# The rows of all engines ordered by the framework's other model, in a two-block transformer kernel

## The chip, the cores and the metric

The kernel runs on one core of a Trainium2 chip. The metric is device microseconds (us) of one execution. Times before: 2521.05, 2525.29 and 2524.74 us, median 2524.74.

## The reference

One sequence of 512 tokens with 1024 features goes through two blocks in float32:

```
first_block:  h = rms_norm(x); q, k, v, bg, cg, xc = split(h @ w_in)
              y_attn = chunked attention with relative bias and QK-norm (16 heads of 64)
              y_conv = bg * conv3(cg * xc)
              x += (sig(gates) * y_attn @ w_attn_proj + sig(gates) * y_conv @ w_conv_proj) @ w_out
              x += square(relu(rms_norm(x) @ w_up)) @ w_down
second_block: shift, scale, gate = split(silu(c) @ w_ada)
              stick-breaking attention (8 heads) and mLSTM (4 heads) side by side, then w_out_2
              PEER: top 16 of 128 x 128 experts for 8 heads; y = sum gate * gelu(h . u_e) * v_e
```

## The kernel before, in words

Activations lie feature-major: 8 tiles of 128 features by 512 tokens. Every float32 operand of a product is split into a rounded high part and a low part, and each product is three matmuls (`mm3`, lines 152 to 156: high-high, high-low, low-high) with 512 columns, 24 per output tile of 128 features (`linear`, line 158). Weights come in blocks of 1 MB: `weights` (line 136) loads a block into `wraw` on the SP queue (line 140), ACT casts it to `whi` (line 143) and DVE, or GpSimd for some blocks, subtracts to `wlo` (lines 145, 149). There are two buffers of each, and in the experts three of `whi` and `wlo` and two of `wraw`.

The stages, in the order of the code: `block1` (line 264) with the convolution branch, `attention` (line 556), the merge with the gates, and the MLP (`w_up`, `w_down`); `mix` (line 665) with `stick_breaking` (line 821) and `mlstm` (lines 921, 955); `peer` (line 1040) with the choice of experts (`select`, line 1238), the spreading of their gates over a table of all 16384 experts for the first 384 tokens (`spread`, line 1302), and `experts` (line 1363), which for these tokens runs through all experts in 128 chunks of 128. The last 128 tokens take another way: `row_experts` (line 1155) gathers the rows of each chosen expert by indirect DMA (line 1152, six buffers) and multiplies them on DVE (lines 1173, 1181) beside the chunks. The activations of the first 48 chunks are computed earlier (`ahead`, line 1111), between the steps of `select` and `spread`.

In the attention each head has four blocks of queries: PE makes scores into PSUM (line 596), DVE adds the bias and takes the maximum (line 598), ACT takes the exponential (line 110, called from `attention`), DVE scales (line 606), PE transposes (line 616), ACT and DVE split (lines 620, 621) and PE multiplies with the values (lines 550, 551). In stick-breaking, PE makes scores (lines 837, 839), ACT takes the absolute value, exponential and logarithm (lines 844, 110), DVE adds and splits (lines 847, 850, 851), PE adds the cumulative sums (lines 864 to 866), ACT takes the exponential (line 110), DVE splits the weights (lines 871, 872) and PE takes the values (lines 550, 551).

What sets the order: the code is traced from top to bottom without an order of its own for the engines. When the `with tile.TileContext(nc)` block (line 1554) closes, the framework makes the rows: it runs the traced program on a model of the chip, and each time an engine is free in that model it gives it, of the instructions that are possible then, the one that was traced first. Buffers are given out in the same run. The outcome is one fixed row per engine and DMA queue, which the chip then executes. So an instruction can be put ahead of many that were traced before it, if the model holds those back. The kernel limits this in places with edges that order two instructions without a wait: `behind` (line 115) adds one. The sums for `w_ada` (line 483) and the products of gathered rows (`later`, line 1160) are kept behind `self.pace`, an instruction of the main work that was traced shortly before them; the transposes that start `spread` are kept behind the last matmul of `ahead` (line 1321), and three early weight loads behind the load of an activation (line 142).

```
mm(out, wh, xh, start=start, stop=False)
mm(out, wh, xl, start=False, stop=False)
return mm(out, wl, xh, start=False, stop=stop)
...
kind = mybir.DependencyClass.Sync if sync else mybir.DependencyClass.NoSync
self.tc.add_manual_dep(i.ins, name, mybir.DependencyInfo(kind, mybir.DependencyReason.DATA), reason="keeps pace")
```

## Time and profile before

| what | value |
|---|---|
| median of 3 runs | 2524.74 us |
| the profiled execution's own time | 2522.37 us |
| its span, first to last instruction | 2520.6 us |
| TensorE (PE) matmuls busy | 2467.9 us, 98% |
| TensorE weight loads (PEld) busy | 2114.4 us, 84% |
| VectorE (DVE) busy | 1872.7 us, 74% |
| ScalarE (ACT) busy | 1056.6 us, 42% |
| GpSimd (POOL) busy | 624.1 us, 25% |
| DMA | 515 MB, mean 204 GB/s |

Busy time is the time in which an engine had at least one instruction in work; matmuls overlap, so the mean length of one is longer than its share of the busy time. The span is what the profile covers, and the execution's own time is 1.8 us longer. SP is the engine that issues most transfers; a wait of "SPq" is one of its queue.

### The profile page before, as it was taken

How to read it: one execution, taken by the hardware profiler on the slowest of the kernel's cores; microseconds unless marked ns; L12 is line 12 of the kernel's file. 1: busy time of each engine (PE TensorE's matmuls, PEld its weight loads, DVE VectorE, ACT ScalarE, POOL GpSimd, SP SyncE). 2: the span in 40 equal slices, each digit the busy share in tenths (PEclk: the TensorE clock that was granted, in tenths of full speed). 3: DMA queues.
4: the chain of work that ended last, by engine and by line, in shares of the span. 5: the costliest groups of instructions: out<-in, count | busy, mean ns of one | idle time of the engine just before them, and what ended most of it. 6: DMA issues, size and time to landing. Idle time of an engine off the chain costs nothing.

```text
span 2520.6 us, 33112 instructions
## 1 busy us (share of the span) xinstructions
PE 2467.9 (98%) x12655; PEld 2114.4 (84%) x12655; DVE 1872.7 (74%) x3094; ACT 1056.6 (42%) x1480; POOL 624.1 (25%) x506
## 2 busy tenths in 40 slices
PE   9999999999999999999999989999999999999999
PEld 7887887877888887777789988978889999999998
DVE  5558777855555557897779999857668787888887
ACT  5226555643222236766653345543333333333332
POOL 0001100111011001001035630011135555555552
PEclk9999999999999999999999999999999999999999
DMA  5352323443444332114343357799879999999995
GB/s 202 127 199 99 104 93 101 139 170 135 174 150 148 138 137 85 38 67 138 120 162 120 124 184 276 311 319 341 300 267 333 327 339 333 328 336 335 336 340 195
DMA packets 172312, 515.03 MB, mean 204 GB/s; under 512 B 13396, under 2 KB 78308, under 8 KB 146296
## 3 DMA queue, kind: packets, MB, share of 16 engines
q1 hardware_dynamic: 133960, 376.52, 42.6%
q0 software_dynamic: 37040, 135.35, 14.9%
q8 instruction: 99, 1.62, 0.2%
q10 hardware_dynamic: 1152, 1.05, 0.1%
q14 instruction: 61, 0.50, 0.1%
HBM read 461.47 MB, written 51.38 MB: 203 GB/s over the span
## 4 chain that ended last, share of the span: by engine, by line
PE 76%; DVE 15%; ACT 4%; DMA 2%; issue 2%; SPq 0%; POOL 0%; ACTq 0%; DVEq 0%; POOLq 0%
PE pa L154 12%; PE pa L156 12%; PE pa L155 12%; PE pp L1443 7%; PE pp L1442 7%; PE pp L1446 7%; PE pu L154 4%; PE pu L156 4%; PE pu L155 4%; DVE wlo L145 1%; ACT whi L143 1%; DVE tk_rest L1194 1%; PE pb L596 1%; DVE tk_e L1230 1%; DMA mg_a<-g_dram 1%
## 5 line engine op out<-in xcount | busy, mean ns | idle before, releaser
L143 ACT CAST whi<-wraw 128x2048 fp32r<-128x2048 f32 x229 | 437.6, 1911 | 540.6 <-PE pa L155 296.5
L145 DVE TENSOR_TENSOR wlo<-wraw,whi 128x2048 fp32r<-128x2048 f32 x210 | 489.0, 2329 | 125.7 <-ACT whi L143 119.3
L154 PE MATMUL pa<-hh,whi 128*128 128x512 f32 (+1 forms) x1360 | 523.0, 385 | 7.1 <-ACT whi L296 3.4
L156 PE MATMUL pa<-hh,wlo 128*128 128x512 f32 (+1 forms) x1360 | 516.4, 381 | 2.3 <-DVE wlo L145 2.2
L155 PE MATMUL pa<-lh,whi 128*128 128x512 f32 (+1 forms) x1360 | 518.4, 381 | 0.0
L1443 PE MATMUL pp<-wlo,hew 128*128 128x512 f32 x768 | 299.0, 390 | 1.5 <-DVE wlo L145 1.5
L1442 PE MATMUL pp<-whi,hew 128*128 128x512 f32 x768 | 298.7, 390 | 1.7 <-ACT hew L1409 1.1
L1152 POOL DMA_INDIRECT r_row<-in_u_rows,r_at x128 | 184.4, 1440 | 461.7 <-DVE r_w L1173 419.6
L154 PEld LDWEIGHTS pa<-hh,whi 128*128 128x128 f32 x1360 | 257.6, 190 | 47.0 <-ACT whi L296 3.6
L156 PEld LDWEIGHTS pa<-hh,wlo 128*128 128x128 f32 x1360 | 257.2, 189 | 44.6 <-issue 3.6
L155 PEld LDWEIGHTS pa<-lh,whi 128*128 128x128 f32 x1360 | 257.5, 189 | 40.9 <-issue 5.3
L1446 PE MATMUL pp<-whi,lew 128*128 128x512 f32 x768 | 237.1, 389 | 0.0
L1152 POOL DMA_INDIRECT r_row<-in_expert_v,r_at x128 | 194.0, 1516 | 173.2 <-DVE r_big L1181 135.7
L156 PE MATMUL pu<-hh,wlo 128*128 128x384 f32 x640 | 215.0, 336 | 0.0
L154 PE MATMUL pu<-hh,whi 128*128 128x384 f32 x640 | 215.0, 336 | 0.0
L155 PE MATMUL pu<-lh,whi 128*128 128x384 f32 x640 | 214.9, 336 | 0.0
L1446 PEld LDWEIGHTS pp<-whi,lew 128*128 128x128 f32 x768 | 144.1, 188 | 30.3
L1443 PEld LDWEIGHTS pp<-wlo,hew 128*128 128x128 f32 x768 | 144.1, 188 | 29.6 <-DVE wlo L145 2.3
L1442 PEld LDWEIGHTS pp<-whi,hew 128*128 128x128 f32 x768 | 144.1, 188 | 29.2 <-ACT hew L1409 1.3
L1181 DVE SCALAR_TENSOR_TENSOR r_big<-r_row,r_w,r_big 128x1024 f32<-128x1024 f32 x127 | 162.9, 1283 | 3.0
L1409 ACT CAST hew<-ex_w 128x384 fp32r<-128x384 f32 x128 | 65.5, 513 | 226.3 <-DVE ex_w L1405 149.1
L1173 DVE CUSTOM_DVE_ANT_0 r_row<-r_row,r_big 128x1024 f32<-128x1024 f32 x128 | 151.3, 1220 | 0.0
(440 smaller groups left out, 4480.1 us busy)
## 6 DMA issues: line engine op xcount, KB each, us to landing
wraw<-in_expert_u SPq DMA_DIRECT2D x64, 1024.0 KB, 7.4
wraw<-in_expert_v SPq DMA_DIRECT2D x64, 1024.0 KB, 7.6
wraw<-in_w_in SPq DMA_DIRECT2D x37, 1024.0 KB, 4.9
ada_w<-in_w_ada SPq DMA_DIRECT2D x24, 1024.0 KB, 4.8
gate_dram<-oh_s SPq DMA_DIRECT2D x12, 2048.0 KB, 7.0
ex_g<-gate_dram SPq DMA_DIRECT2D x31, 768.0 KB, 10.9
wraw<-in_w_up SPq DMA_DIRECT2D x16, 1024.0 KB, 5.3
wraw<-in_w_down SPq DMA_DIRECT2D x16, 1024.0 KB, 4.8
```

Source lines behind the costliest of these rows:

```text
L143: nc.scalar.copy(hi, raw)
L145: nc.vector.tensor_sub(lo, raw, hi.bitcast(F32))
L154: mm(out, wh, xh, start=start, stop=False)
L155: mm(out, wh, xl, start=False, stop=False)
L156: return mm(out, wl, xh, start=False, stop=stop)
L1152: self.nc.gpsimd.indirect_dma_start(t, None, src, at)
L1173: later(nc.vector.tensor_tensor_reduce(row, row, h, 1.0, 0.0, op0=ALU.mult, op1=ALU.add, accum_out=w[:, k:k + 1]))
L1181: later(nc.vector.scalar_tensor_tensor(acc, row, w[:, k:k + 1], acc, op0=ALU.mult, op1=ALU.add))
L1409: nc.scalar.copy(hi, w)
L1442: mm(sums[b][half], hi, v[0][:, c, hc], start=n == 0, stop=False)
L1443: mm(sums[b][half], hi, v[1][:, c, hc], start=False, stop=False)
L1446: mm(sums[b][half], lo, v[0][:, c, hc], start=False, stop=n == P - 1)
```

## The change

It gives the context that makes the rows one more argument, by which the program is run on the framework's timeline model instead of its default one. Kernel code, instructions, operands, buffers' numbers and edges stay. What can differ is the sequence in each engine's row and in each DMA queue, and the buffer that a tile gets.

```diff
--- before.py
+++ after.py
@@ -1551,7 +1551,7 @@
     I = {n: nc.dram_tensor("in_" + n, a.shape, mybir.dt.from_np(a.dtype), kind="ExternalInput").ap()
          for n, a in A.items()}
     y = nc.dram_tensor("out_y", (T // P, P, D), F32, kind="ExternalOutput").ap()
-    with tile.TileContext(nc) as tc:
+    with tile.TileContext(nc, schedule_with_timeline_sim=True) as tc:
         build(tc, I, y)
     r = run_bass_kernel_spmd(nc, [{"in_" + n: a for n, a in A.items()}], core_ids=[0])
     return np.ascontiguousarray(r.results[0]["out_y"].reshape(1, T, D))
```

## Rows read from the trace of the kernel before

**Rows 1.** The page's head, busy time, and the granted clock in 40 slices.

```profile
span 2520.6 us, 33112 instructions
...
PE 2467.9 (98%) x12655; PEld 2114.4 (84%) x12655; DVE 1872.7 (74%) x3094; ACT 1056.6 (42%) x1480; POOL 624.1 (25%) x506
...
PEclk9999999999999999999999999999999999999999
```

**Rows 2.** Busy time by stage: stretch, its length, busy us (instructions) of each engine.

```profile
core 0: us, PE busy (x) PEld busy (x) DVE busy (x) ACT busy (x) POOL busy (x), PEclk, DMA share, GB/s
0.00:190.00 190.00, 185.58 (x808) 152.93 (x809) 109.67 (x132) 62.59 (x66) 13.73 (x22) 0.99 0.49 177
190.00:500.00 310.00, 304.48 (x1610) 247.88 (x1610) 242.12 (x530) 177.97 (x349) 33.62 (x62) 1.00 0.30 103
500.00:600.00 100.00, 95.24 (x402) 75.59 (x400) 51.43 (x57) 43.21 (x52) 11.19 (x8) 0.98 0.50 180
600.00:940.00 340.00, 340.00 (x1493) 279.96 (x1492) 186.21 (x208) 87.85 (x79) 40.17 (x32) 1.00 0.40 144
940.00:1275.00 335.00, 316.62 (x1611) 254.98 (x1611) 267.73 (x416) 219.82 (x381) 28.79 (x36) 0.99 0.28 96
1275.00:1485.00 210.00, 206.17 (x1121) 188.63 (x1119) 190.71 (x869) 80.34 (x95) 118.18 (x90) 1.00 0.39 131
1485.00:1655.00 170.00, 162.08 (x1391) 149.20 (x1392) 143.46 (x128) 87.09 (x147) 9.07 (x6) 0.96 0.73 279
1655.00:2521.00 866.00, 857.78 (x4228) 765.20 (x4227) 681.36 (x757) 297.70 (x314) 369.31 (x250) 1.00 0.90 318
```

**Rows 3.** What TensorE waits for: total us, times, longest.

```profile
PE pb L1319 <- DVE pk_i L1236: 6.8, 1, 6.8
PE pd L550 <- DVE sb_wh L871: 5.7, 2, 3.4
PE pb L596 <- DVE at_st L598: 3.5, 4, 0.9
```

**Rows 4.** Busy time and granted clock of two stretches of 20 us.

```profile
1020.00:1040.00 20.00, 19.05 (x122) 16.64 (x120) 19.38 (x37) 15.31 (x28) 0.00 (x0) 1.00 0.16 54
1040.00:1060.00 20.00, 17.09 (x86) 13.64 (x86) 14.09 (x23) 11.68 (x21) 0.00 (x0) 0.91 0.08 22
```

**Rows 5.** Groups of instructions in the attention, 190 to 500 us: the softmax.

```profile
L110 ACT ACTIVATE at_e<-at_e,at_st 128x128 f32<-128x128 f32 (+1 forms) x64 | 35.9, 563 | 17.6 <-DVE at_st L600 17.5
...
L598 DVE CUSTOM_DVE_ANT_0 at_e<-pb,bias 128x128 f32<-128x128 f32 (+1 forms) x64 | 29.3, 481 | 0.9 <-PE pb L596 0.7
...
L606 DVE TENSOR_SCALAR at_e<-at_e,at_r 128x128 f32<-128x128 f32 (+1 forms) x64 | 21.1, 386 | 0.1
```

**Rows 6.** Groups of instructions in the mixer, 940 to 1275 us: stick-breaking.

```profile
L110 ACT ACTIVATE sb_l<-sb_l 128x512 f32<-128x512 f32 (+1 forms) x48 | 27.3, 592 | 0.6
...
L847 DVE SCALAR_TENSOR_TENSOR sb_l<-pb,sb_l 128x512 f32<-128x512 f32 (+1 forms) x24 | 15.1, 638 | 2.4 <-ACT sb_l L110 2.2
...
L844 ACT ACTIVATE sb_l<-pb 128x512 f32<-128x512 f32 (+1 forms) x24 | 13.2, 557 | 6.0 <-DVE sb_o L851 5.2 <-PE pb L839 0.8
L110 ACT ACTIVATE sb_w<-pb 128x512 f32<-128x512 f32 (+1 forms) x24 | 13.1, 554 | 1.6 <-DVE sb_wl L872 1.6
...
L871 DVE CAST sb_wh<-sb_w 128x512 fp32r<-128x512 f32 (+1 forms) x24 | 9.1, 394 | 0.0
```

**Rows 7.** Groups of instructions in the experts, 1660 to 2500 us.

```profile
L145 DVE TENSOR_TENSOR wlo<-wraw,whi 128x2048 fp32r<-128x2048 f32 x103 | 235.9, 2290 | 75.5 <-ACT whi L143 74.5
...
L143 ACT CAST whi<-wraw 128x2048 fp32r<-128x2048 f32 x103 | 197.0, 1913 | 190.3 <-PE pp L1446 86.2 <-PE pu L155 80.4 <-DMA wraw<-in_expert_v 21.8
...
L1181 DVE SCALAR_TENSOR_TENSOR r_big<-r_row,r_w,r_big 128x1024 f32<-128x1024 f32 x127 | 162.9, 1283 | 3.0
```

**Rows 8.** The page's DMA issues: size and us from issue to landing.

```profile
wraw<-in_expert_v SPq DMA_DIRECT2D x64, 1024.0 KB, 7.6
```

**Rows 9.** What DVE waits for in the experts, 1660 to 2500 us.

```profile
DVE wlo L145 <- ACT whi L143: 74.5, 60, 5.0
```

## The prediction

> **What bounds the kernel now.** I read the page's head first, then busy time by stage, then what TensorE waits for, and last the groups of the stages that wait. In the head [rows 1] the reader is to see one number: PE is busy for 2467.9 of 2520.6 us. TensorE is the bound, and 2520.6 - 2467.9 = 52.7 us is all that stands between the span and a TensorE that never rests. The change removes no instruction, so these 52.7 us are the only time that an order can give back, and it has no such limit in the other direction.
>
> The table by stage [rows 2] shows where the 52.7 us lie. From 600 to 940 us, the first block's MLP, PE is busy for 340.00 of 340. From 1655 us to the end, the experts, 857.8 of 866, and part of the missing 8.2 is the end itself. These two stages are 1206 us in which the order has next to nothing to give. Idle time sits in the others: 4.4 us at the start, 5.5 in the attention (190 to 500), 4.8 in the merge (500 to 600), 18.4 in the mixer (940 to 1275), 3.8 in the expert selection, 7.9 in the spreading of its gates (1485 to 1655). The waits [rows 3] name the longest of them: 6.8 us in one piece for the last index of the selection, a chain that no order shortens; 5.7 us in two pieces for the weights of stick-breaking; 3.5 us in four pieces for the running maximum of the attention. So the time sits in hand-offs: PE makes scores, ACT and DVE work on them, PE takes them up again, and other matmuls have to stand in the row meanwhile.
>
> **What the change does.** It adds and removes no instruction, no wait of the algorithm, no transfer. It changes the rows, that is, the sequence in which every engine and every DMA queue gets its instructions. Program order is the priority in both cases, and the NoSync edges (`behind`) hold in both; between instructions that are both possible, the model's clock decides which comes first. An engine takes its row strictly in sequence, so an instruction whose operand is late holds up all behind it. I cost it stage by stage.
>
> MLP and start: nothing. The work that covers any shift is there: DVE is busy for 186 of 340 us and ACT for 88 [rows 2], so both have slack of over 45% and weights are split long before PE wants them. If that cover went, one late split would cost at most one cast and one subtraction, 1.91 + 2.29 us by their groups in the experts [rows 7].
>
> Attention: one softmax block costs 0.481 us on DVE (score plus bias, with maximum), 0.563 us on ACT (exponential) and 0.386 us on DVE (scaling) [rows 5]: 1.43 us from PE to PE, 64 times. Fully hidden it costs nothing; fully exposed, 64 x 1.43 = 91.5 us. Now 5.5 us of it are exposed, 6%.
>
> Mixer: one stick-breaking block costs 0.557 + 2 x 0.592 us on ACT, 0.638 us on DVE (the cast after it is left out as partly parallel), then 0.554 on ACT and 0.394 on DVE before its values are taken [rows 6]: 3.33 us, 24 times, 79.8 us if nothing hid it. The whole mixer now has 18.4 us idle.
>
> Together the two stages could expose 91.5 + 79.8 = 171.3 us and expose 5.5 + 18.4 = 23.9, 14%. No row of before shows what share another order exposes. The ends are 0 (everything hidden: -23.9 us) and 171.3 (+147 us). I take the value nearest to the rows and on the wider side: a share twice as large, 28%, so +23.9 us. The reason is the asymmetry just shown: from 14% there is little way down and much way up, and the fillers that hide a hop (projections for the next group) are a fixed stock, so an order that spends them earlier in one place lacks them in another.
>
> The clock adds to it. Between 1020 and 1040 us, where PE was busy for 19.05 of 20, the granted clock was 1.00; between 1040 and 1060, where it was busy for 17.09, it was 0.91 [rows 4], part of the stretch at 1.2 GHz instead of 2.4. At 0.91, 20 us lose 0.09 x 20 = 1.8 us. I count one such stretch more, +1.8 us.
>
> Merge, selection and spreading: 4.8 + 3.8 + 7.9 us idle, of which 6.8 are the fixed chain. I put the change at zero here, bounded by -9.7 (all that is not that chain) and +9.7.
>
> Experts: 0 in the forecast. Here the DMA queue is part of what is moved. Each weight block is loaded in 7.6 us [rows 8], cast by ACT in 1.91 and subtracted by DVE in 2.29 [rows 7]: 11.8 us for one of two raw buffers. 103 blocks go through in the 840 us of that view, 8.16 us each, so a buffer may take 16.3 us for its turn, and 4.5 us are slack. That slack is what hides a shift of DVE's row; the third rival below says what it costs without.
>
> The sum: 2522.4 us (the profiled execution's own time) + 23.9 + 1.8 = 2548.1, so 2548. The median of the runs shown is 2524.74, 2.4 us above the profiled one; I leave that inside the range.
>
> A rule that speaks for more room than I give: the Trainium skill, "Perfetto Trace Analysis", section "Identifying the Most-Contended Engine", says that busy time of matmuls is not a good measure for TensorE's distance from its peak and that the busy share of weight loads is better. That share is 84% here, so by that rule 406 us would be open, and a better order could bring the kernel far below 2468. The trace does not agree: in the MLP, where PE waits for nothing, weight loads are busy for 280 of 340 us, 82% [rows 2], so 84% over the span is what this mix of matmuls gives when it is full. I give that outcome under 1 in 100, and the sum stays.
>
> **The rivals.** First, faster. The one mechanism is the mixer's pair of stalls on the stick-breaking weights and those around them: if the new rows put another projection, or the next head's scores, ahead of the values matmul, its idle falls. It decides when over a third of the mixer's idle goes without new idle in the attention. Price: half of 18.4 and half of the spreading's 7.9 is -13 us, and a clock stretch less is -1.8: about 2507. The whole of the mixer, the spreading and the attention would be -31.8 us, 2491. For it: the kernel's PE is in fact idle while other engines work, and a different clock in the model may see these stalls. Against it: PE was handed over to fillers well in 94 to 98% of those stages, and each filler moved is missing elsewhere.
>
> Second, no change that can be measured (within 0.2%, 5 us; about what a measurement of this kernel can tell from none): the two models agree wherever it matters, because program order and the edges hold, or gains in the mixer are paid for in the attention. That the option would leave the rows as they are belongs here: 2522 to 2525.
>
> Third, slower by more, through the experts. DVE takes its row in order: it stood still for 74.5 us in 60 waits for ACT's cast ahead of a subtraction [rows 9]. The Trainium skill, "TensorE: Matmul & The Clock Gate", section "Architectural detail", says the same of ACT and DVE, and that TensorE itself only pulls weight loads ahead. If the new row puts row products (1.28 us each [rows 7]) ahead of the subtraction, the raw buffer comes free later. Up to three fit into the 4.5 us of slack; with five, 6.4 us, each turn of a buffer is 1.9 us too long. 103 / 2 turns make 98 us: 2620. It decides from the fourth product on. Against it: the NoSync edges keep the products behind a chunk's last split, and six gathered rows at most can be ready.
>
> **How the numbers follow.** Forecast (slower by the hand-offs, 2530 to 2600): 0.38. Faster, 2490 to 2519: 0.35, of which 0.08 below 2502. No change: 0.15. Slower through the experts: 0.12, of which half above 2605; with 0.04 of the forecast's own tail, 0.10 lies above that. So 2502 to 2605 leaves out 0.18. As both signs hold much of the chance: the likeliest case alone reaches from 2530 to 2600. Faster by over 0.2%: 0.35; within: 0.15; slower: 0.38 + 0.12 = 0.50.
>
> **What the profile after would show.** Right: PE busy still about 2468, the MLP still 340 of 340, the idle of attention and mixer together near 48 us instead of 23.9, with the same waits (maximum and stick-breaking weights) longer and more often, and one or two more stretches at 1.2 GHz. Wrong in size: the same waits with another share. Wrong in kind: the mixer's idle below 12 us with the attention's unchanged (first rival); or PE in the experts waiting for the subtracted weights by tens of us, with the load queue waiting for it longer than now (third rival); or rows that are the same as before.

## The result and the profile after

The changed kernel takes 2603.77 us (median of 4 runs, 2603.08 to 2605.75), the kernel before beside it 2524.04 us (2521.05 to 2525.29). The ratio is 1.0319, with an interval of 1.0304 to 1.0335: slower by 79.7 us. The profiled execution took 2603.89 us. The page's head, which answers to [rows 1]:

```profile
span 2602.1 us, 33125 instructions
...
PE 2491.0 (96%) x12655; PEld 2141.7 (82%) x12655; DVE 1873.5 (72%) x3094; ACT 1063.3 (41%) x1480; POOL 632.0 (24%) x506
...
PEclk9999999899999999997989999989999999999999
```

The counts are those of before, and DVE and ACT are busy for the same time to within 1%. The span grew by 81.5 us. PE's busy time grew by 23.1 us with the same 12655 matmuls, and PE's idle time from 52.7 to 111.1 us, by 58.4. So two things are to be found: 58 us of waits, and 23 us in which matmuls ran slower. The clock's row has its first figures below 9. The mean granted clock is 0.978, against 0.995. As it has two levels, 1.2 and 2.4 GHz, that is 2 x 0.022 x 2602.1 = 114 us at 1.2 GHz, against 25 us before. By the clock's records PE is busy for 75 of these 114 us, and before it was for 25. At the lower level the same matmuls take about twice as long: in the trace of before those of 384 columns start every 0.17 us at 1476 us (granted clock 1.00) and every 0.32 us at 1489 (0.50). So 50 us more of busy time at 1.2 GHz are worth some 25 us, about the 23.1 that PE's busy time grew by.

The table by stage, cut where the work of each stage ends in this trace (start, attention, merge with MLP, mixer, selection, spreading, experts):

```profile
core 0: us, PE busy (x) PEld busy (x) DVE busy (x) ACT busy (x) POOL busy (x), PEclk, DMA share, GB/s
0.00:187.00 187.00, 182.52 (x794) 150.71 (x795) 105.75 (x128) 60.79 (x65) 13.88 (x22) 1.00 0.50 177
187.00:520.00 333.00, 311.52 (x1602) 257.11 (x1601) 244.71 (x531) 181.94 (x348) 34.12 (x62) 0.97 0.27 93
520.00:964.00 444.00, 441.31 (x1924) 361.73 (x1925) 237.91 (x267) 131.91 (x133) 51.61 (x40) 1.00 0.44 155
964.00:1327.00 363.00, 322.75 (x1595) 262.79 (x1594) 265.96 (x410) 219.84 (x377) 28.25 (x36) 0.92 0.24 83
1327.00:1554.00 227.00, 211.75 (x1128) 191.17 (x1127) 196.35 (x878) 84.89 (x100) 115.89 (x90) 0.98 0.37 129
1554.00:1738.00 184.00, 162.84 (x1390) 152.22 (x1391) 142.78 (x127) 86.46 (x145) 9.05 (x6) 0.93 0.69 260
1738.00:2602.00 864.00, 858.35 (x4230) 765.96 (x4228) 680.10 (x756) 297.46 (x314) 379.19 (x250) 1.00 0.90 318
```

The stages of [rows 2] were cut at round times. The same view of before, cut at the same points of the work, gives for attention, mixer, selection and spreading:

```profile
187.00:495.00 308.00, 302.48 (x1602) 246.23 (x1601) 242.08 (x531) 177.88 (x350) 33.62 (x62) 1.00 0.29 100
...
942.00:1271.00 329.00, 312.44 (x1597) 252.21 (x1596) 263.83 (x410) 216.79 (x376) 28.79 (x36) 0.99 0.28 94
1271.00:1488.00 217.00, 208.41 (x1129) 189.84 (x1127) 197.50 (x881) 84.96 (x100) 118.18 (x90) 1.00 0.39 131
1488.00:1657.00 169.00, 162.93 (x1395) 149.73 (x1396) 141.58 (x124) 87.43 (x148) 9.07 (x6) 0.96 0.74 283
```

Side by side, with the idle time of PE in each stage:

| stage | length before, after | PE busy before, after | PE idle before, after |
|---|---|---|---|
| start | 187, 187 | 182.6, 182.5 | 4.4, 4.5 |
| attention | 308, 333 | 302.5, 311.5 | 5.5, 21.5 |
| merge and MLP | 447, 444 | 442.2, 441.3 | 4.8, 2.7 |
| mixer | 329, 363 | 312.4, 322.8 | 16.6, 40.3 |
| selection | 217, 227 | 208.4, 211.8 | 8.6, 15.3 |
| spreading | 169, 184 | 162.9, 162.8 | 6.1, 21.2 |
| experts | 863, 864 | 856.9, 858.4 | 6.1, 5.7 |

Four stages lost 25, 34, 10 and 15 us. The stages in which PE is full did not move. What PE waits for, the longest, against [rows 3]:

```profile
PE pd L550 <- DVE sb_y L554: 10.3, 2, 7.1
PE pb L1319 <- DVE pk_i L1236: 10.2, 1, 10.2
PE pu L1107 <- DMA xc<-x_dram: 9.8, 4, 9.2
PE pb L154 <- ACT if_h L774: 6.7, 1, 6.7
PE pa L154 <- ACT hmx L181: 6.4, 1, 6.4
PE pb L801 <- DVE if_b L792: 5.9, 1, 5.9
PE pd L550 <- DVE at_y L554: 5.7, 6, 2.1
PE pb L596 <- DVE at_st L598: 5.5, 3, 3.3
```

Of the three kinds in [rows 3], the selection's last index went from 6.8 to 10.2 us, the running maximum from 3.5 to 5.5, and the stick-breaking weights left the top. New, or grown from about 1 us, are single waits of 6 to 9 us, each for the end of one chain while PE stands: the addition that empties the accumulator of stick-breaking's values (`sb_y`), the split weights and the values of the mLSTM's gates (`if_h`, `if_b`), the operand of the mixer's output projection (`hmx`), the reload of `x` (1.2 us in all before). The steps of the chains cost what they did. The groups of the softmax, which answer to [rows 5]:

```profile
L110 ACT ACTIVATE at_e<-at_e,at_st 128x128 f32<-128x128 f32 (+1 forms) x64 | 35.7, 559 | 39.1 <-DVE at_st L600 38.9
L598 DVE CUSTOM_DVE_ANT_0 at_e<-pb,bias 128x128 f32<-128x128 f32 (+1 forms) x64 | 30.4, 485 | 17.2 <-PE pb L596 16.4 <-PE pc L616 0.5
...
L606 DVE TENSOR_SCALAR at_e<-at_e,at_r 128x128 f32<-128x128 f32 (+1 forms) x64 | 20.5, 383 | 0.4
```

The mean durations, 559, 485 and 383 ns, are within 1% of before. The idle times in front of them are not: ACT waits 38.9 us for the maximum where it waited 17.5, and DVE 16.4 us for scores from PE where it waited 0.7. The engines wait for each other in turn. Stick-breaking, against [rows 6], reads the same way (595 ns for the logarithm, 561 for the weights, and DVE's 5.5 us of waits ahead of L847 where there were 2.2).

Where such a bare stretch lies, windows show. The first two lines are the end of the attention, the next two the middle of the mixer, the last the end of the spreading:

```profile
460.00:483.00 23.00, 23.00 (x96) 17.71 (x95) 19.24 (x25) 12.98 (x20) 1.22 (x2) 1.00 0.36 126
483.00:520.00 37.00, 25.58 (x107) 19.27 (x106) 30.93 (x97) 23.60 (x59) 6.18 (x12) 0.74 0.17 53
...
1170.00:1178.00 8.00, 4.01 (x25) 3.52 (x23) 6.16 (x9) 4.90 (x7) 0.00 (x0) 0.93 0.30 96
1178.00:1201.00 23.00, 11.00 (x24) 7.22 (x25) 8.80 (x14) 5.86 (x9) 0.00 (x0) 0.51 0.44 155
...
1718.00:1738.00 20.00, 9.10 (x37) 6.26 (x38) 1.27 (x3) 5.42 (x11) 0.00 (x0) 0.66 0.84 286
```

From 460 to 483 us PE is full: these 96 matmuls are the last group's gate projections, the fillers. From 483 to 520 the last heads run without any, PE is busy for 25.58 of 37 us, and the granted clock is 0.74. In TensorE's row 104 matmuls of the attention stand behind the last gate projection, where before there was none. The mixer has the worst stretch: PE busy for 4.01 of 8 us, and then 23 us almost wholly at 1.2 GHz (0.51).

Counted in TensorE's row, the fillers of the attention stood before in 111 runs of 8.6 matmuls on average (3 of 20 or more) between matmuls of heads. Now there are 56 runs of 17.0 (17 of 20 or more). This is the same stock in larger blocks. The spreading shows it too, in the trace: before, at most 29 one-hot matmuls stand in one run between preparing ones, and some 90 preparing matmuls behind the last of them cover the load of `x`; now the last 253 stand in one run, with no preparing matmul behind them.

The experts, against [rows 7] and [rows 9], did not change:

```profile
L145 DVE TENSOR_TENSOR wlo<-wraw,whi 128x2048 fp32r<-128x2048 f32 x103 | 236.0, 2291 | 71.9 <-ACT whi L143 71.1 <-issue 0.7
...
L1181 DVE SCALAR_TENSOR_TENSOR r_big<-r_row,r_w,r_big 128x1024 f32<-128x1024 f32 x127 | 162.8, 1282 | 2.3
```

### The profile page after: what moved, and what is told of

It is laid out like the page before. It is cut to its first block, busy times and chain, and to the rows that moved or that the text cites. A ratio compares the mean times of both kernels' runs of the same rounds, so it can differ in the third digit from the quotient of the medians.

```text
span 2602.1 us, 33125 instructions
## 1 busy us (share of the span) xinstructions
PE 2491.0 (96%) x12655; PEld 2141.7 (82%) x12655; DVE 1873.5 (72%) x3094; ACT 1063.3 (41%) x1480; POOL 632.0 (24%) x506
## 4 chain that ended last, share of the span: by engine, by line
PE 85%; DVE 11%; ACT 2%; DMA 1%; issue 1%; POOL 0%; SPq 0%; ACTq 0%; DVEq 0%; POOLq 0%
PE pa L154 15%; PE pa L155 15%; PE pa L156 15%; PE pp L1443 7%; PE pp L1446 7%; PE pp L1442 7%; PE pu L154 4%; PE pu L156 4%; PE pu L155 4%; DVE tk_rest L1194 1%; PE pd L510 1%; PE pb L596 1%; PE pd L550 1%; DVE wlo L145 1%; DVE tk_e L1230 1%
## 5 line engine op out<-in xcount | busy, mean ns | idle before, releaser
L1152 POOL DMA_INDIRECT r_row<-in_expert_v,r_at x128 | 207.0, 1617 | 161.4 <-DVE r_big L1181 132.1
L1181 DVE SCALAR_TENSOR_TENSOR r_big<-r_row,r_w,r_big 128x1024 f32<-128x1024 f32 x127 | 162.8, 1282 | 2.3
```

The costliest lines, as they stand in the source:

```text
L1152: self.nc.gpsimd.indirect_dma_start(t, None, src, at)
L1181: later(nc.vector.scalar_tensor_tensor(acc, row, w[:, k:k + 1], acc, op0=ALU.mult, op1=ALU.add))
```

## The experiments

The first four had three theories. **Theory A**: the timeline model hands an engine instructions ahead of time, up to 35 for TensorE and 12 for the others (its table of queue depths), and what is handed over can't be overtaken; so fillers go into TensorE's row early and in blocks. **Theory B**: the other terms of that model (its durations, for instance) make the order worse. **Theory C**: TensorE's row is not the cause, but how the rows of the other engines stand to it. "Pinned" means below that a row is put in a given sequence by edges without a wait, one from each instruction to the next:

```diff
+def pin(tc, rows):
+    traced = {i.name: i for i in tc.nc.cur_bb.bb.instructions}
+    dep = mybir.DependencyInfo(mybir.DependencyClass.NoSync, mybir.DependencyReason.DATA)
+    for text in rows:
+        row = [n for n in _row(text) if n in traced]
+        for a, b in zip(row, row[1:]):
+            tc.add_manual_dep(traced[b], a, dep, reason="row")
```

**1. TensorE handed 2 instructions ahead.**

```diff
+    TRN2Spec.ENG_ISSUE_QUEUE_DEPTH = {**TRN2Spec.ENG_ISSUE_QUEUE_DEPTH, mybir.EngineType.PE: 2}
     with tile.TileContext(nc, schedule_with_timeline_sim=True) as tc:
```

> The rows are made on the timeline model, as after, but in the model PE may have 2 instructions handed out and not yet finished, where the model by itself lets it run many ahead. Theory A (the model hands PE its matmuls many at a time and early, so that fillers are taken in blocks ahead of attention, mixer and spreading work and are missing at the seams): 2510 to 2550 us, the attention's last projection for the gates is again at its end, and PE's idle falls from 111 us to under 70. Theory B (the model's durations and latencies, not its window, make the worse rows): 2580 to 2615 us. Theory C (the rows of DVE, ACT and SP cost the time, not PE's): 2580 us or more, as those are still made on the timeline model.

Measured: 2534.39 us, ratio to before 1.0047 (1.003 to 1.0064). That is 11.9 us above the kernel before beside it, where the changed kernel is 79.7 above: 68 us went with one number of the model. The filler runs of the attention are 105 of 9.3 matmuls. The attention and the mixer of this run, by busy time, and then what PE waits for longest:

```profile
188.00:489.00 301.00, 297.18 (x1602) 251.86 (x1601) 242.16 (x531) 178.60 (x348) 38.72 (x62) 0.99 0.30 103
...
942.00:1286.00 344.00, 316.21 (x1594) 255.87 (x1592) 264.08 (x410) 217.67 (x377) 28.80 (x36) 0.96 0.25 87
```

```profile
PE pu L1107 <- DMA xc<-x_dram: 9.9, 4, 9.2
PE pb L154 <- ACT if_h L774: 7.1, 1, 7.1
PE pb L801 <- DVE if_b L792: 5.9, 1, 5.9
```

The attention takes 301 us, 7 less than before the change, with 3.8 us of PE idle. The mixer takes 344, 15 more than before, because the mLSTM's gate chain is bare here too. The wait for `x` is as long as in the changed kernel, and yet selection and spreading together take 383 us against 386 before: this wait alone is not what made the spreading longer (the wait for the selection's last index, 6.8 us before, is 0.6 us in this run).

**2. All engines handed 2 ahead.**

```diff
+    TRN2Spec.ENG_ISSUE_QUEUE_DEPTH = {e: 2 for e in TRN2Spec.ENG_ISSUE_QUEUE_DEPTH}
```

> As the run before, with a window of 2 for every engine in the model. Theory A: 2505 to 2550 us, within 1% of the run with PE alone, as PE is the engine with the long stock of possible work. If the windows of DVE and ACT matter as much (theory C), it is over 1% faster than the run with PE alone. Theory B: 2580 to 2615 us.

Measured: 2535.43 us, ratio 1.0052 (1.0035 to 1.0069), the same as with TensorE alone. At this depth of TensorE's, those of the other engines make no difference.

**3. TensorE handed 8 ahead**, the same edit with 8 in the place of 2.

> The timeline order with TensorE handed 8 instructions ahead instead of 35 (2604 us) or 2 (2534 us). Theory A with a dose: the length of the filler runs follows the depth (in TensorE's row of attention 96 runs of 10.1 matmuls here, 56 of 17.0 at 35, 105 of 9.3 at 2), so the time lies between, 2540 to 2565 us, and nearer to 2. If the depth matters only because anything beyond the next instruction is wrong, 2590 to 2604 us. If 35 is an accident of one order and any other depth is good, 2530 to 2538 us.

Measured: 2544.08 us, ratio 1.0086 (1.007 to 1.0102). So 2, 8 and 35 give 2534, 2544 and 2604 us, with mean filler runs of 9.3, 10.1 and 17.0 matmuls. The order is the one that theory A needs.

**4. TensorE's row pinned to that of before, the others left to the timeline.**

```diff
     with tile.TileContext(nc, schedule_with_timeline_sim=True) as tc:
         build(tc, I, y)
+        pin(tc, ROWS)
```

> Rows made on the timeline model, as after, with PE's row alone held by edges to the sequence of the kernel before; the other engines' rows come out as the timeline model has them. Theory A and theory B (PE's row carries the loss): 2520 to 2545 us. Theory C (the others' rows carry it): 2575 us or more.

Measured: 2590.16 us, ratio 1.0272 (1.0255 to 1.029). Although TensorE's row is the good one, 68 us are lost. What PE waits for longest in the attention of this run:

```profile
PE pb L596 <- DVE at_st L598: 13.2, 8, 3.0
PE pb L596 <- DVE at_st L600: 4.1, 4, 1.2
```

The scores of the next block wait for DVE's eviction of the one before. That fits a row of TensorE that asks for it at a point at which VectorE's row does not yet have it.

**5. The other way round: the default model, TensorE's row pinned to that of after**, with the same lines in the kernel before.

> Rows made on the default model, as before, with PE's row alone held by edges to the sequence of the kernel after. Theory A and theory B (PE's row carries the loss): 2580 to 2610 us. Theory C: 2525 to 2550 us.

Measured: 2621.77 us, ratio 1.0394 (1.0377 to 1.0411). With other rows made for it by the default model, the row in blocks costs 99 us, more than in the kernel it comes from.

**6. The rows of the four other engines pinned to those of before, TensorE's left to the timeline.**

> The timeline order with TensorE's row left to it and the rows of VectorE, ScalarE, GpSimd and SyncE in the sequence of the kernel before. TensorE's row then has its fillers in still longer blocks (43 runs of 23.2 matmuls in attention, against 111 of 8.6 before and 56 of 17.0 after). Theory A (blocks of fillers in TensorE's row cost the time by themselves): 2585 to 2640 us. Theory J alone (VectorE's row decides, TensorE's follows): 2525 to 2560 us.

Measured: 2718.03 us, ratio 1.0774 (1.0756 to 1.0792), worse than either end that the two theories gave. This is the kernel before with TensorE's row alone replaced, by one with the fillers in 43 runs of 23.2, and it loses 194 us. Its attention by busy time, and what PE waits for there:

```profile
187.00:603.00 416.00, 347.65 (x1604) 276.05 (x1603) 238.03 (x529) 175.95 (x347) 32.62 (x62) 0.90 0.21 71
```

```profile
PE pa L154 <- DVE qn_n L500: 21.4, 4, 5.4
PE pa L156 <- DVE wlo L145: 14.0, 10, 1.7
PE pa L154 <- ACT whi L143: 11.1, 6, 2.9
```

PE, at the start of a projection, waits 21.4 us for DVE to empty the accumulator of a projection (`qn_n`), and 25.1 us for weights to be split. These operations stand in DVE's and ACT's rows where TensorE's finer row of before needed them. The attention takes 416 us instead of 308, and 45 of these 108 us are longer busy time (347.65 us against 302.5), at a granted clock of 0.90.

**7. TensorE's row pinned to before, and every engine handed 2 ahead.** Both edits together ask whether the depth of the others made the loss of experiment 4.

> The timeline model with every engine handed 2 instructions ahead, and TensorE's row put in the sequence of the kernel before. With the usual depth for the others (12) the same row of TensorE ran 2590.2 us. Theory G (that loss came from the other engines' depth: with 12 they too take work in too early against a row that is not theirs): 2525 to 2545 us. Theory H (a row of TensorE that is imposed always fits the other rows badly, whatever their depth; the rows must be made with one another): 2575 to 2600 us.

Measured: 2587.39 us, ratio 1.026 (1.0244 to 1.0277). It did not; theory G falls.

**8. TensorE's and VectorE's rows pinned to before.**

> The timeline order, with TensorE's and VectorE's rows put in the sequence of the kernel before; ScalarE, GpSimd and SyncE stay by the timeline. With TensorE's row alone it ran 2590.2 us, and there TensorE's longest kind of wait in attention was for VectorE's eviction of scores (13.2 us in 8 waits). Theory J (VectorE's row is the other half: evictions that TensorE waits for stand behind work that is not urgent): 2520 to 2540 us. Theory K (every engine's row carries a share): 2550 to 2580 us.

Measured: 2569.13 us, ratio 1.0179 (1.0162 to 1.0196).

**9. All rows but VectorE's pinned to before.**

> The timeline order with only VectorE's row left to it, and the rows of TensorE, ScalarE, GpSimd and SyncE in the sequence of the kernel before. Theory J: VectorE's row alone keeps most of the loss of the run with TensorE's row imposed, 2570 to 2595 us. Theory K: a part of it, 2535 to 2565 us. If ScalarE's row was the cause: 2520 to 2535 us.

Measured: 2563.06 us, ratio 1.0152 (1.0135 to 1.0169). Both runs are where theory K has them. VectorE's row in the sequence of the timeline costs 39 us although all others are right, and again the attention shows it:

```profile
PE pb L596 <- DVE at_st L598: 9.5, 7, 1.8
PE pd L551 <- DVE pt2l L621: 4.3, 4, 1.1
```

With VectorE's row right as well as TensorE's, 45 us stay, which ScalarE's, GpSimd's and SyncE's rows make between them; which of these three was not tried, and pins between rows that the model fills differently may add to it.

**10. Fillers held back.** A direct test of "too early": the last group's gate projections are tied to the values of heads 11 to 14, and the last 96 preparing matmuls to the end of the one-hot matmuls.

```diff
-                        pg = self.linear(gw, j, hs)
+                        pg = self.linear(gw, j, hs, after=self.values[11 + 2 * (n2 % 2) + j] if g == 3 else None)
...
+                    if g >= NS // 2 - 2 and k == 0:
+                        self.behind(mm, self.oh)
```

> The timeline order as it is (TensorE handed 35 instructions ahead), with two kinds of filler held back by ordering edges: each of the last group's four gate projections may begin only behind the first value matmul of heads 11, 12, 13 and 14, and the last 96 matmuls that prepare the experts only behind the last one-hot matmul. Theory A (fillers are put into TensorE's row too early, so that the end of attention and the load of the experts' x stand bare): the last attention matmul ends at 495 to 508 us instead of 520.4, the wait of TensorE for the x tiles (9.2 us) falls below 2 us, and the whole is 20 to 30 us faster, 2574 to 2584 us. Theory F (the holes there come from late softmax and stick-breaking answers by the other engines' rows, and fillers in another place only move them): 2596 to 2608 us, with attention again ending past 515 us.

Measured: 2620.89 us, ratio 1.0386 (1.037 to 1.0402), slower than the changed kernel by 17 us. Neither theory had this. The first line is the whole attention of this run, the second the stretch in which the held fillers used to be, the third its spreading, and then what PE waits for in the spreading:

```profile
187.00:533.00 346.00, 313.83 (x1605) 258.32 (x1604) 245.98 (x531) 182.57 (x348) 35.08 (x62) 0.96 0.26 89
465.00:492.00 27.00, 12.56 (x33) 7.12 (x31) 22.94 (x52) 15.46 (x32) 6.82 (x8) 0.62 0.13 48
1573.00:1757.00 184.00, 163.75 (x1381) 153.75 (x1381) 141.79 (x125) 85.94 (x142) 9.07 (x6) 0.92 0.68 259
```

```profile
PE pd L1355 <- DVE oh_h L1347: 6.4, 2, 3.7
PE pb L1355 <- DVE oh_h L1347: 3.3, 2, 2.7
...
PE pu L1113 <- DMA xc<-x_dram: 1.8, 4, 0.8
```

(Lines of this kernel stand up to 8 lower.) The fillers do stand between the last heads now. But from 465 to 492 us PE is busy for 12.56 of 27, at a clock of 0.62: the hole has only moved forward, and grew. The wait for `x` fell from 9.8 to 1.8 us as wanted, and the spreading still takes 184 us, as in the changed kernel. The 96 matmuls are still in it (1381 matmuls, 163.75 us busy), nearly all behind the last one-hot matmul, so that 277 one-hot matmuls now stand in one run in front of them, and PE waits longer for the one-hot operands (`oh_h` 6.4 and 3.3 us, where it was 2.7 and 2.7). "Too early" is the wrong half of theory A, as far as these blocks show: moving some of them, in a set of rows that is otherwise kept, gave nothing back.

**11. The mixer alone put back.** The changed kernel, with the rows of all five engines of before, for the mixer only.

> The changed kernel, with the rows of all five engines for the mixer alone put in the sequence of the kernel before. In the changed kernel the mixer took 363 us against 329. If the loss of a stage is made in its own rows: 34 us come back, all of them, 2566 to 2576 us. If a late or bare neighbour stage carries part of it in (buffers, weights, a clock that is low at the start of the stage): 2580 to 2600 us.

Measured: 2572.37 us, ratio 1.0201 (1.0184 to 1.0218), 31.4 us less than the changed kernel. The merge with the MLP, and the mixer:

```profile
520.00:964.00 444.00, 441.05 (x1925) 360.95 (x1926) 238.01 (x268) 131.88 (x133) 51.65 (x40) 1.00 0.44 155
964.00:1293.00 329.00, 313.43 (x1595) 252.99 (x1594) 261.32 (x408) 215.88 (x375) 29.12 (x36) 0.98 0.27 91
```

The mixer takes 329 us, as before the change. So its 34 us are made in its own rows, not brought in by a neighbour.

**12. The best parts together.** Experiment 1 with the mixer's rows of before.

> The kernel with TensorE handed 2 instructions ahead (2534.4 us), and for the mixer alone (from its first sequence projection to its last output projection) the rows of all five engines put in the sequence of the kernel before. In it the mixer took 15.8 us more than before, attention 6 us and selection 6 us less. If stages can be put together (rows must agree with one another inside a stage, and little is carried across), the mixer's 15.8 us come back: 2514 to 2522 us, below the kernel before (2522.5 us). If the mixer's loss came with what the stages on either side leave it (buffers, weights loaded late), it stays: 2528 to 2538 us.

Measured: 2521.18 us (2519.39 to 2523.54), before beside it 2522.55, ratio 0.9995 (0.9987 to 1.0004). That is in the first of the two ranges, at its upper end, and not to be told from the kernel before. The attention keeps its gain and the mixer its old length:

```profile
188.00:489.00 301.00, 297.18 (x1602) 251.85 (x1601) 242.08 (x531) 178.65 (x349) 38.80 (x62) 0.99 0.30 103
489.00:940.00 451.00, 444.47 (x1925) 363.51 (x1924) 239.02 (x267) 132.67 (x134) 53.70 (x40) 0.99 0.43 153
940.00:1269.00 329.00, 312.63 (x1595) 252.16 (x1594) 261.89 (x409) 216.31 (x376) 29.46 (x36) 0.99 0.26 90
```

Of the 7 us gained in the attention the merge and MLP give 4 back (451 us against 447, PE idle 6.5 against 4.8 and busy 2.2 longer). No version beat both kernels by more than a measurement can tell.

**What the runs settle.** The depth at which the timeline model hands matmuls out is the cause of 68 of the 79.7 us (experiments 1 to 3). TensorE's row in large blocks is bad with other rows too (5 and 6). That the length of the blocks does it by itself is not shown: the row of before, in short runs, cost 68 us too among rows that were not made with it (4). The loss is a property of the rows together: sets mixed from both orders still lose 39 to 68 us, even with all rows but one from the better order (4, 7 to 9), and later places for a few blocks give nothing back (10). A whole stage, all engines at once, can be put back and returns what it lost (11). **What stays open** is the last 12 us at a depth of 2. In the sum they lie in the mixer (experiment 12 takes them away), but which term of the model puts its fillers there was not tried. Buffers are given out together with the rows, so a run with pinned rows can also have other buffers; no run separates the two.

## Why the prediction was right and wrong

**The sign and what bounds the kernel** were right. PE's idle time was named as the only thing an order can change, small on the way down and open on the way up; it went from 52.7 to 111.1 us. The size was wrong: 79.7 us slower where 24 was forecast. Three terms of the sum failed: the hand-offs of attention and mixer (+23.9, measured 39.7), selection and spreading (0, measured 21.8), and the clock (+1.8, measured 23.1). That the value, 2603.77 us, lies just inside the range of 2502 to 2605 is luck: the case that was forecast was given 2530 to 2600, and what lies above that was mostly the third rival's, which did not come.

**Start, MLP, experts at zero**: right. They took 187, 444 and 864 us against 187, 447 and 863. Of the third rival nothing shows: DVE waited 71.1 us for ACT's cast instead of the 74.5 of [rows 9].

**Attention and mixer, a share twice as large (+23.9 us)**: that hand-offs come to stand bare was right, the term was mis-sized, and the waits were mostly not those that it was made of. The idle time of the two stages went from 22.1 to 61.8 us, by 39.7. That is as much as 36% of the 171.3 us of hand-offs where 28% was taken, and the choice of the factor rested on nothing but a nearness to the rows. Of the two waits named for it one got longer, the maximum (5.5 us against 3.5); the other, the stick-breaking weights, gave way to the ends of chains. Some of these were never in the 171.3 us: the sum for the mixer held stick-breaking blocks alone, and the mLSTM's gates (6.7 and 5.9 us) and the operand of the output projection (6.4) make 19.0 us of PE's waits there now; the sum for a block of the attention ended at the scaling, and PE waits 5.7 us for the addition that empties the values' accumulator (`at_y`). I had multiplied the 64 and 24 blocks by a share, as if every block lost a little; the loss came in a few long holes where the fillers had run out.

**The clock, one stretch more (+1.8 us)**: this is the step that failed by the largest factor. PE's busy time grew by 23.1 us. I had priced a stretch by [rows 4], 20 us at 0.91, and counted one; after, there are 37 us at 0.74, 23 at 0.51 and 20 at 0.66 among others, 114 us at 1.2 GHz in all against 25. Both terms have one cause, which I did not join up: a bare stretch is priced twice, once as PE's idle time and again because the matmuls in it and behind it run at the lower clock.

**Merge, selection and spreading at zero, bounded by 9.7**: the merge with the MLP was right (3 us less). The other two were wrong, and so was the bound. Selection and spreading took 25 us more, of which 21.8 are idle. The idle time that is there says what can be gained, not what can be lost, exactly the asymmetry that I had used for the attention and did not apply here. The spreading is also a chain with fillers in between (the one-hot blocks, and the preparing matmuls). And the 6.8 us of the last index, which the prediction called a fixed chain that no order shortens, are only the part that stood bare: it is 10.2 us after the change, and 0.6 us in experiments 1 and 12.

The sum with what was measured: 39.7 in attention and mixer, 21.8 in selection and spreading, 23.1 of clock, and 3.1 less in the rest, 81.5 us, the growth of the span.

**That the fillers are a fixed stock** was the sentence of the prediction that was borne out best: experiment 10 moved 192 matmuls of them and moved the holes. What it lacked is the size of the blocks. The prediction had no view on how far ahead a model may commit a row, and so no reason to expect more than a factor of two.

**Rows taken strictly in sequence**: the Trainium skill, "TensorE: Matmul & The Clock Gate", section "Architectural detail", calls ACT and DVE strict in sequence, as the prediction said of the third rival. The runs here agree for VectorE, in another place: with its row alone out of step, PE waited 9.5 us in the attention for its evictions of scores, and the kernel lost 39 us (experiment 9).

## What to carry to other kernels

Where one engine is full, cost a new order from both ends: downwards by the idle time in each stage, upwards by the hand-offs that its fillers hide now, in every stage that has such chains, and let each bare stretch count again for the clock. An order that comes from a model is a set of rows made for one another; mixed engine by engine, rows of two orders were never as good here as those of before, and worse than either order where a TensorE row in longer blocks stood among rows of the default model (2622 and 2718 us), while a whole stage could be exchanged and gave back all it had lost. When a model commits a row far ahead, look at the lengths of the filler runs in that row first: 111 runs of 8.6 went with 2524 us and 56 of 17.0 with 2604. They do not decide alone: the same 111 runs among rows that were not made with them went with 2590.

## What the runs showed that was not expected

- TensorE's row alone, replaced in the kernel before by one with longer blocks, cost 194 us (2718.03 us) with the same 12655 matmuls: PE was idle for 2713.7 - 2546.7 = 167.0 us, and its busy time grew by 78.8 us at a mean granted clock of 0.969.
- The wait for the reload of `x` does not tell how long the spreading takes: 184 us with the wait at 9.8 and at 1.8 us (the changed kernel and experiment 10), and 169 us with it at 1.2 and at 9.9 (the kernel before and experiment 12). When it went, other waits came, and the other way round.
- Stages add up to within a few us: the mixer's rows of before gave back 33.6 us of its 34 by the end of the mixer, and 31.4 us of the whole.
